# RWKV-7 hybrid layer: the triangular inverses of two head pairs share their visits to TensorE

## The chip, the cores and the metric

The kernel runs on one core of a Trainium2 chip. The metric is device time in microseconds for one launch. Three runs of the kernel before took 983.35, 985.12 and 985.98 us; the median is 985.12. Its engines are named as in the profile: PE is TensorE (PEld its weight loads), DVE is VectorE, ACT is ScalarE, POOL is GpSimd, SP is the engine that issues most transfers.

## What is computed

One layer of a hybrid decoder, for a prompt of 512 tokens and 8 x 8 sampled tokens (576 columns in all): an RWKV-7 branch and a differential-attention branch on the same normalised input, gated and merged, then a squared-ReLU MLP and a last norm. The change touches the RWKV branch alone. In the reference that branch is a recurrence over tokens on a 64 x 64 state for each of 8 heads:

```python
def step(S, inp):
    r_t, w_t, k_t, v_t, a_t, b_t = inp
    sa = jnp.einsum('bhij,bhj->bhi', S, a_t)
    S = S * w_t[:, :, None, :] + sa[..., None] * b_t[:, :, None, :] + v_t[..., None] * k_t[:, :, None, :]
    return S, jnp.einsum('bhij,bhj->bhi', S, r_t)
...
S, ys = lax.scan(step, S0.astype(jnp.float32), xs)
...
m = gate_a * (o_a @ lp['w_br_a']) + gate_b * (o_b @ lp['w_br_b'])
x = x + m @ lp['w_out']
hn = rmsnorm(x, lp['g_ffn'], NORM_EPS)
x = x + jnp.square(jax.nn.relu(hn @ lp['w_up'])) @ lp['w_down']
```

The kernel takes the tokens in chunks of 64. Within a chunk the recurrence is a triangular system, so for each chunk and head a 64 x 64 unit triangular matrix has to be inverted.

## The kernel before

The eight heads are four head pairs, hp 0 to 3; two heads of a pair lie on the upper and the lower 64 partitions. Pairs 0 and 1 are the first group, 2 and 3 the second; `e` is hp % 2. A group's recurrence over eight chunks is `chain(0)` or `chain(1)`, which needs the inverses of both its pairs.

`rwkv(hp)` is a generator in stages: the set-up up to the masked products A (ABR), then the transposes (SVU, KBt, pI), then the inverse, then what follows the chain. `run(...)` at the end of the phase advances these generators by one stage for each number it is given.

The inverse of a pair works on 9 chunks (8 of the prompt, one of the sampled tokens), as 32 x 32 blocks on the diagonal of the array. It makes four steps l = 1 to 4. Each has a visit with the products pW (from DM and X), an ACT copy W<-pW, a visit with the products pZ (from Y and W), a DVE sum X<-X,pZ and a DVE transpose Y<-X. Steps 1 and 2 take 36 products a visit (9 chunks by 4 blocks), steps 3 and 4 take 32. Two visits of 16 products, pWc and pC, then join the 32 x 32 blocks to the 64 x 64 inverse TT. A product of 32 x 32 in float32 stands as two records of PE and two of PEld in the trace. So a pair makes ten visits, one after the other, and each waits for what ACT or DVE made of the visit before.

To give TensorE work meanwhile, dense products wait in the list `waiting`: the streams of the big projections (ps_z for the RWKV inputs, ps_g for the gates, ps_brb for the attention branch), 128 x 128 weights by 288 or 296 columns. `take(n)` emits n of them, `fill(n)` does so behind the last product written, and `blocks()` took 9 behind each visit of a pair's inverse. They get a late priority, and the scheduler places them after what is due; `tc.issue_after(ins)` ties an instruction behind another on its engine.

Products of the inverse go to the one bank of `tbank`; `bank` is a pool of three banks that the set-up, the transposes and the outputs use. Lines that matter: `mm` (L72) records all these products, `act` is L58, `tt` L61; the transposes of the inverse are L894 and L918; the chain's products are L1021.

## Time and profile before

| what | before |
|---|---|
| median of three runs | 985.12 us |
| the profiled execution | 984.4 us |
| its span | 982.6 us |
| granted TensorE clock | 0.996 |
| DVE busy | 676.1 us, 69% of the span |
| ACT busy | 507.2 us, 52% |
| inverses of the first group, first to last product | 206.5 to 279.4 us |
| inverses of the second group | 381.9 to 431.3 us |

The page gives busy time by engine, the span in slices, the DMA queues and the chain of work that ended last. The trace can be asked for the instructions in order of time (the timeline), for what an engine waited for (the waits view), and for busy time and numbers of instructions in a stretch (the windows). "Issue" in a bracket means that an engine stood idle and nothing in the profile released it. A name such as pZ<-W,Y is the tile written and the tiles read.

### The profile page before, as it was taken

To read this page: it belongs to the slowest core of one execution; us is meant where nothing else is said; L and a number is where in the kernel's file an instruction comes from. 1 tells how busy PE (TensorE), PEld (TensorE's weight loads), DVE (VectorE), ACT (ScalarE), POOL (GpSimd) and SP (SyncE) were. 2 spreads that over 40 slices of the span, in tenths; PEclk is the share of its full clock that TensorE was granted. 3 is DMA by queue.
4 is the path that set the end of the run, shared out by engine and by line. 5 is a ranking of instruction groups with operands and counts; after the bars stand their busy time and mean duration, and the time that the engine had idled before them with its cause. 6 is when DMAs were issued, how large, how long until landed. Compare 5 with 4: busy or idle time off the path is not lost.

```text
span 982.6 us, 24623 instructions
## 1 busy us (share of the span) xinstructions
PE 951.1 (97%) x10120; PEld 898.2 (91%) x10120; DVE 676.1 (69%) x1427; ACT 507.2 (52%) x1120; POOL 72.8 (7%) x181
## 2 busy tenths in 40 slices
PE   8999999999999998999999999999999999999996
PEld 8999989887978997878899999999999999999996
DVE  6698566875556848354787989966666666666744
ACT  6576455565345464543354767444444444444732
POOL 2611100100010210001300000000000000000001
PEclk9999999999999999999999999999999999999998
DMA  7422663201212225221477532222222232220402
GB/s 267 141 71 72 207 222 118 86 26 45 67 57 77 94 88 190 70 83 58 173 239 234 179 121 86 87 86 87 86 87 87 90 93 93 92 86 23 140 1 97
DMA packets 50833, 105.75 MB, mean 108 GB/s; under 512 B 6066, under 2 KB 8114, under 8 KB 50594
## 3 DMA queue, kind: packets, MB, share of 16 engines
q1 hardware_dynamic: 47442, 96.95, 30.6%
q0 software_dynamic: 1648, 5.35, 1.6%
q10 hardware_dynamic: 1632, 1.89, 0.6%
q8 instruction: 79, 1.29, 0.5%
q14 instruction: 32, 0.26, 0.1%
HBM read 89.38 MB, written 14.78 MB: 106 GB/s over the span
## 4 chain that ended last, share of the span: by engine, by line
PE 56%; DVE 2%; ACT 1%; DMA 1%; issue 1%; POOL 0%; DVEq 0%
PE ps_dn L72 20%; PE ua L1261 5%; PE ux L1261 5%; PE ps_wo L72 4%; PE ps_g L72 4%; PE ps_brb L72 3%; PE ps_bra L72 3%; PE uc L1261 3%; PE ub L1261 3%; PE ud L1261 2%; PE pch L1021 2%; DMA raw_dn<-in_w_down_dram 1%; PE pW L72 1%; PE pZ L72 0%; DVE ya L61 0%
## 5 line engine op out<-in xcount | busy, mean ns | idle before, releaser
L72 PE MATMUL ps_dn<-q,hi_dn 128*128 128x288 f32 x768 | 154.7, 296 | 0.0
L72 PEld LDWEIGHTS ps_dn<-q,hi_dn 128*128 128x128 f32 x768 | 122.8, 188 | 1.5
L72 PE MATMUL ps_dn<-q,lo_dn 128*128 128x288 f32 x384 | 113.2, 295 | 0.0
L72 PE MATMUL ps_g<-xh,hi_g 128*128 128x288 f32 x256 | 77.7, 303 | 1.0 <-DVE gg L61 1.0
L72 PE MATMUL ps_g<-xh,lo_g 128*128 128x288 f32 x256 | 78.5, 307 | 0.0
L72 PE MATMUL ps_g<-xl,hi_g 128*128 128x288 f32 x256 | 78.2, 305 | 0.0
L72 PEld LDWEIGHTS ps_dn<-q,lo_dn 128*128 128x128 f32 x384 | 72.0, 188 | 0.0
L72 PE MATMUL ps_z<-xh,lo_z 128*128 128x288 f32 (+1 forms) x224 | 69.7, 311 | 0.0
L72 PE MATMUL ps_z<-xl,hi_z 128*128 128x288 f32 (+1 forms) x224 | 67.2, 300 | 0.0
L72 PE MATMUL ps_z<-xh,hi_z 128*128 128x288 f32 (+1 forms) x224 | 67.1, 299 | 0.0
L61 DVE TENSOR_TENSOR ya<-ya,ps_dn 128x288 f32<-128x288 f32 x96 | 43.3, 451 | 27.6 <-PE ps_dn L72 27.5
L58 ACT ACTIVATE hi_dn<-raw_dn 128x512 fp32r<-128x512 f32 x48 | 30.1, 628 | 56.2 <-PE ps_dn L72 56.1
L58 ACT ACTIVATE c<-c 128x288 f32<-128x288 f32 x112 | 48.7, 439 | 9.4 <-DVE c L61 7.7
L1261 PE MATMUL ux<-h_t,hi 128*128 128x288 f32 x256 | 52.4, 297 | 0.0
L1261 PE MATMUL ua<-h_b,hi 128*128 128x288 f32 x256 | 52.2, 296 | 0.0
L72 PEld LDWEIGHTS ps_g<-xh,hi_g 128*128 128x128 f32 x256 | 48.2, 188 | 2.5 <-issue 1.4
L72 PEld LDWEIGHTS ps_g<-xl,hi_g 128*128 128x128 f32 x256 | 48.2, 188 | 1.8 <-issue 0.5
L58 ACT ACTIVATE hi<-a 128x1024 fp32r<-128x1024 f32 (+1 forms) x32 | 27.1, 846 | 43.3 <-PE ps_dn L72 34.9
L72 PEld LDWEIGHTS ps_g<-xh,lo_g 128*128 128x128 f32 x256 | 48.1, 188 | 1.4
L72 PE MATMUL ps_dn<-q,w 128*128 128x320 f32 (+1 forms) x336 | 46.6, 298 | 0.8 <-DVE fin L61 0.8
L72 PEld LDWEIGHTS ps_dn<-q,w 128*128 128x128 f32 x336 | 45.3, 190 | 1.2 <-DVE fin L61 1.1
L61 DVE TENSOR_TENSOR lo<-s,hi 128x1024 fp32r<-128x1024 f32 x32 | 39.2, 1224 | 10.4 <-ACT hi L58 10.3
(390 smaller groups left out, 2730.6 us busy)
## 6 DMA issues: line engine op xcount, KB each, us to landing
a<-in_w_up_dram SPq DMA_DIRECT2D x32, 512.0 KB, 3.3
raw_dn<-in_w_down_dram SPq DMA_DIRECT2D x64, 256.0 KB, 2.8
raw_g<-in_w_in_dram SPq DMA_DIRECT2D x32, 256.0 KB, 3.1
raw_z<-in_w_in_dram SPq DMA_DIRECT2D x28, 256.0 KB, 2.9
gt_d<-gg SPq DMA_DIRECT2D x16, 288.0 KB, 2.8
g<-gt_d SPq DMA_DIRECT2D x16, 288.0 KB, 3.7
kp<-in_ktab_dram SPq DMA_DIRECT2D x16, 256.0 KB, 3.5
vp<-in_vtab_dram SPq DMA_DIRECT2D x16, 256.0 KB, 3.5
```

The source lines that it names most:

```text
L58: ring["act"] = AE.activation(out=out, in_=in_, func=func, **kw)
L61: ins = (eng or VE).tensor_tensor(out=out, in0=a, in1=b, op=op)
L72: ring["mm"] = PE.matmul(out=out, lhsT=lhsT, rhs=rhs, start=start, stop=stop)
L1021: ring["mm"] = PE.matmul(out=ps[rows, e], lhsT=lhs, rhs=rhs, start=first and e == 1, stop=True, skip_group_check=True)
L1261: ring["mm"] = PE.matmul(out=ps[:, :288], lhsT=l[:, k], rhs=hb[blk][:, h, k], start=start and i == 0, stop=i == 11, skip_group_check=skip)
```

## The change

The inverse leaves `rwkv` and becomes a generator of its own, `inverse(...)`, which yields after each visit. `rwkv` only makes it, at the end of its transposes. `invert(*steps)` advances the inverses of the pairs named in each step by one visit and then emits 9 dense products behind the last small one. With `(0,)` a visit is of pair 0 alone; with `(0, 1)` both pairs' products are written one behind the other. `tied` puts each product of the second pair behind the first pair's last one. The second pair's products use `bank`, not `tbank`.

For each group the steps are four for the even pair alone, then the odd pair's set-up, then seven with both, then four for the odd pair. The even pair has no products left in the seventh, so six visits are shared: pW of step 3 with pW of step 1 and so on to pC with pZ of step 3. The dense products taken between the two set-ups are 136 in the first group, which were 146; behind pWc and pC, too, nine are now taken.

```diff
+    visit = {}
+
+    def tied(*args):
+        with tc.issue_after(visit["last"].ins) if visit.get("last") else nullcontext():
+            last = mm(*args)
+        visit["lead"] = visit.get("lead") or last
+
+    def inverse(own, e, hp, dn, ST, KBt, ABR, pc):
+        tb = tbank if e == 0 else bank
...
+        def blocks(ps, lhs, rhs, n):
+            for ci in range(n):
+                for g in range(4):
+                    gs = slice(32 * g, 32 * g + 32)
+                    tied(ps[gs, ci * 32:ci * 32 + 32], lhs[gs, ci], rhs[gs, ci])
+            return ps[:, :n * 32].rearrange("p (c s) -> p c s", c=n)
+
+        for l in range(1, 5):
...
+            pW = blocks(tb(f"pW{hp}{l}"), DM, X, n)
+            yield
+            act(W[:, :n], pW)
+            pZ = blocks(tb(f"pZ{hp}{l}"), Y, W, n)
+            yield
+            tt(X[:, :n], X[:, :n], pZ, ADD)
...
+    def invert(*steps, dense=9):
+
+        for step in steps:
+            visit.clear()
+            for hp in step:
+                lead = visit.pop("lead", None)
+                if lead is not None:
+                    visit["last"] = ring["mm"]
+                next(pair[hp // 2]["inv", hp % 2], None)
+            with tc.issue_after(ring["mm"].ins):
+                take(dense)
+
...
-            act(W[:, :n], blocks(tbank(f"pW{hp}{l}"), DM, X, n))
-            tt(X[:, :n], X[:, :n], blocks(tbank(f"pZ{hp}{l}"), Y, W, n), ADD)
...
-        own[e] = ST, KBt, TT, ABR, pc
+        own["inv", e] = inverse(own, e, hp, dn, ST, KBt, ABR, pc)
         yield
...
     run(0, 0)
     take(101)
-    run(0, 1, 1)
-    take(146)
-    run(1)
+    invert(*[(0,)] * 4)
+    run(1, 1)
+    take(136)
+    invert(*[(0, 1)] * 6, *[(0, 1)], *[(1,)] * 4, dense=9)
     chain(0)
     run(0, 1, 2)
     take(310)
     run(2, 3)
     take(85)
-    run(2, 0, 1, 3)
+    invert(*[(2,)] * 4)
+    run(0, 1, 3)
     take(18)
-    run(3)
+    invert(*[(2, 3)] * 7, *[(3,)] * 4, dense=9)
```

On TensorE the first two visits of head pair 1 stood alone before, in the first group (pW and pZ are the small products, ps_z the dense ones):

```order
L72 MATMUL ps_z_1_3952<-xl,hi_z_1_3947 128x296
L72 MATMUL pW_4012<-X_4004,DM_1_4009 32x32 x36
L72 MATMUL ps_z_1_3952<-xh,lo_z_1_3948 128x296
...
L72 MATMUL ps_z_0_4074<-xl,hi_z_0_4066 128x288
L72 MATMUL pZ_4082<-W_1_4011,Y_4003 32x32 x36
L72 MATMUL ps_z_0_4074<-xh,lo_z_0_4067 128x288
```

The same two visits of pair 1 on TensorE now, with pair 0's third step in front of each (its W is W_3, its X and Y are X_3098 and Y_3097):

```order
L72 MATMUL ps_z_1_3685<-xl,hi_z_1_3680 128x296
L72 MATMUL pW_3736<-X_3098,DM_3_3733 32x32 x32
L72 MATMUL pW_3783<-X_3776,DM_1_3780 32x32 x36
L72 MATMUL ps_z_1_3685<-xh,lo_z_1_3681 128x296
...
L72 MATMUL ps_z_0_3845<-xl,hi_z_0_3837 128x288
L72 MATMUL pZ_3853<-W_3_3735,Y_3097 32x32 x32
L72 MATMUL pZ_3887<-W_1_3782,Y_3775 32x32 x36
L72 MATMUL ps_z_0_3845<-xh,lo_z_0_3838 128x288
```

Nine dense products stand between two visits in both orders; a visit now holds 68 products in a row where it held 36.

On VectorE, behind the first visits of pZ of pair 1, the order before was (X1 and Y1 are pair 1's; numbers behind a tile's name tell pair and step, DM the masked factor of a coming step):

```order
L61 TENSOR_TENSOR X1_4004<-X1_4004,pZ11_4082 128x288
L918 STREAM_TRANSPOSE Y1_4003<-X1_4004 128x288
L61 TENSOR_TENSOR DM1_4_4341<-DT1_3997,cst_sb_75 128x256
L61 TENSOR_TENSOR X1_4004<-X1_4004,pZ12_4180 128x288
L61 TENSOR_TENSOR Z11_4060<-ps_z11_0_4074,R1_108 128x288
```

and is now, with pair 0's X0 and Y0 in the same burst:

```order
L61 TENSOR_TENSOR X0_3098<-X0_3098,pZ03_3853 128x256
L790 STREAM_TRANSPOSE Y0_3097<-X0_3098 128x256
L61 TENSOR_TENSOR X1_3776<-X1_3776,pZ11_3887 128x288
L790 STREAM_TRANSPOSE Y1_3775<-X1_3776 128x288
L61 TENSOR_TENSOR DM1_3_4128<-DT1_3769,cst_sb_75 128x256
```

The sum and the transpose of pair 1 now stand behind those of pair 0, two sums and two transposes to a visit.

## The prediction

> **What bounds the kernel now.** I read the page first: the busy row, the chain, the DMA queues.

> ```profile
> PE 951.1 (97%) x10120; PEld 898.2 (91%) x10120; DVE 676.1 (69%) x1427; ACT 507.2 (52%) x1120; POOL 72.8 (7%) x181
> PE 56%; DVE 2%; ACT 1%; DMA 1%; issue 1%; POOL 0%; DVEq 0%
> q8 instruction: 79, 1.29, 0.5%
> ```

> TensorE is busy for 97% of the span and is what the chain is made of. So an edit moves the time only if TensorE does its fixed list of products in less time, or stands idle for less. The third row becomes important further down.

> Then the timeline of TensorE around single visits of the 32x32 products, since the change is about those. Columns: start, duration, what ran, how many, and in brackets the idle time ahead of it.

> ```profile
> 415.04 0.29 PE L72 MATMUL ps_g<-xh,hi_g 128*128 128x288 f32 x1
> 415.26 0.82 PE L72 MATMUL pW<-X,DM 32*32 32x32 f32 x72
> 416.01 0.41 PE L72 MATMUL ps_g<-xl,hi_g 128*128 128x288 f32 x1
> 416.26 0.29 PE L72 MATMUL ps_g<-xh,lo_g 128*128 128x288 f32 x1
> 416.39 0.29 PE L72 MATMUL ps_g<-xh,hi_g 128*128 128x288 f32 x1
> ...
> 417.18 0.29 PE L72 MATMUL ps_g<-xh,hi_g 128*128 128x288 f32 x1
> 417.40 0.75 PE L72 MATMUL pZ<-W,Y 32*32 32x32 f32 x65
> 418.77 0.26 PE L72 MATMUL pZ<-W,Y 32*32 32x32 f32 x7 [0.61 <-issue]
> 418.96 0.40 PE L72 MATMUL ps_g<-xl,hi_g 128*128 128x288 f32 x1
> ```
> ```profile
> 422.20 0.29 PE L72 MATMUL ps_g<-xh,hi_g 128*128 128x288 f32 x1
> 422.43 0.75 PE L72 MATMUL pZ<-W,Y 32*32 32x32 f32 x64
> 423.11 0.40 PE L72 MATMUL ps_g<-xl,hi_g 128*128 128x288 f32 x1
> 423.35 0.30 PE L72 MATMUL ps_g<-xh,lo_g 128*128 128x288 f32 x1
> ```
> ```profile
> 227.52 0.30 PE L72 MATMUL ps_z<-xl,hi_z 128*128 128x296 f32 x1
> 227.75 0.69 PE L72 MATMUL pC<-Y,Wc 32*32 32x32 f32 x32
> 228.37 0.40 PE L72 MATMUL ps_z<-xh,lo_z 128*128 128x296 f32 x1
> 228.61 0.30 PE L72 MATMUL ps_z<-xh,hi_z 128*128 128x296 f32 x1
> ```

> Dense products start 0.13 us apart (416.26 to 416.39; nine take 1.2 us). From the last dense start before a visit to the second dense start after it: 1.22 us with 72 records of small products (36 products, two records each), 1.15 us with 64. Eight records make the difference of 0.07, so one costs 0.00875 us. Of the 1.15 us, 64 records are 0.56 and the two dense steps 0.27; **0.32 us is the visit itself**, the price of leaving the dense stream and coming back. The visit of pC takes 1.09: less 0.27 and 0.32, its 32 records (other corners of the array) cost 0.50 us.

> **A second limit.** Inside the visit at 417.40 TensorE stops after 65 records and nothing releases it but "issue". I asked the waits view for all of these, and the windows between their ends:

> ```profile
> PE pZ L72 <- issue: 1.9, 3, 1.0
> ...
> 387.31:391.07 3.76, 2.74 (x142) 2.44 (x139) 2.23 (x6) 0.74 (x2) 0.00 (x0) 1.00 0.51 163
> 415.42:418.77 3.35, 2.73 (x146) 2.44 (x139) 0.43 (x1) 0.41 (x1) 0.00 (x0) 1.00 0.31 84
> 422.77:426.43 3.66, 3.37 (x149) 2.78 (x135) 2.47 (x5) 2.01 (x5) 0.00 (x0) 1.00 0.28 92
> 216.64:219.63 2.99, 2.99 (x130) 2.50 (x128) 2.83 (x6) 1.33 (x3) 0.00 (x0) 1.00 0.02 5
> ```
> ```profile
> 391.07:418.77 27.70, 26.33 (x765) 23.69 (x765) 10.68 (x22) 14.58 (x39) 0.00 (x0) 1.00 0.24 71
> 418.77:426.43 7.66, 7.37 (x255) 6.37 (x255) 4.00 (x8) 3.47 (x8) 0.00 (x0) 1.00 0.15 46
> 265.94:268.97 3.03, 3.03 (x129) 2.65 (x130) 1.24 (x3) 0.00 (x0) 0.00 (x0) 1.00 0.02 5
> ```
> ```profile
> q8 instruction: 1, 0.02, 5.8%
> ```

> The counts in brackets are records of TensorE and of its weight loads. Between the ends of the gaps at 391.07 and 418.77 lie 765 + 765 of them, six times 256 within the records cut at the edges; between 418.77 and 426.43, 255 + 255, twice 256. And 79 instruction packets against 20,240 records on the page are 256 records each. So TensorE's program arrives in blocks of 256, and it stops at a block's edge when the next has not come. The last row is of the DMA view for 388.5 to 389.8 us: one packet, 5.8% of 16 engines over 1.3 us, 1.2 us long; the gap it belongs to ended at 391.07, 1.3 us after that window. The first four windows each run from one edge to the next, where TensorE waited: a refill took 3.76, 3.35, 3.66 and 2.99 us. The fifth, 3.03 us, is a block passed without a gap, so its refill took at most that. Nothing in the traces shows two refills under way at once. Mean of the five: 3.36 us.

> **The change part by part.** The profiled execution took 984.4 us (span 982.6), 0.7 under the median of 985.12.

> *Fewer visits.* Ten visits a head pair, 40, become 28: in each group four alone, six shared, four alone. Twelve fewer at 0.32 us: **-3.8 us**. No product goes away. The chain and the head-pair set-up meet other dense products than before (the order has three fewer excursions to the chain, a few more to transposes and A blocks); I take 0, within 1 us both ways.

> *Waits on other engines.* Of the dependency waits of the inverses only one of the two of pWc, head pair 0's, falls into a shared visit and goes:

> ```profile
> PE pW L72 <- DVE X L61: 1.6, 2, 1.2
> PE pWc L72 <- DVE X L61: 0.4, 2, 0.2
> ```

> The 1.6 us are in visits that stay alone, the first steps of head pairs 0 and 2, with the same VectorE work ahead of them. **-0.2 us**; -2.0 if they all go, and 0 if this one only moves.

> *Tied products.* The small products of a visit stand in one run already (x72, x64), so the ties cost and save 0. The second pair's products use the shared banks, not the one bank kept for them; nobody waits for a bank in the rows, so 0.

> *Supply of the shared stretch.* This is the term that decides. Four shared visits hold 32 + 36 products, 136 records on TensorE and as many weight loads; two hold 16 + 32, 96 and 96. With nine dense products (18 records) between them the stretch has 4x272 + 2x192 + 5x18 = 1562 records, 6.1 blocks. Unhindered it takes 4x(0.32 + 136x0.00875) + 2x(0.32 + 0.50 + 64x0.00875) + 5x1.2 = 14.8 us, **2.43 us a block: faster than any refill seen**. Alone, a visit of 64 and its dense products are 146 records in 2.1 us, 3.6 us a block, just above the 3.36; that is why only a few gaps are in the trace now. At the start of a stretch the current block (half of it on average) and the next one are there; 4.6 blocks have to be waited for, each 3.36 - 2.43 = 0.93 us: 4.3 us a group, **+8.6 us** for both. At 2.99 us it is 5.2, at 3.76 it is 12.2, and 0 if a refill can come in 2.43.

> *The gaps of today.* The three issue gaps sum to 1.9 us of idle; each costs some 0.2 more than its idle (the visit at 417.40 lasts 1.56 us to the next dense product, against 0.75 for the one at 415.26: 0.81 for 0.61 idle), and a fourth, inside this row, costs 0.2 against the 0.75 of its like:

> ```profile
> 218.97 0.97 PE L72 MATMUL pZ<-W,Y 32*32 32x32 f32 x64
> ```

> Together 2.7 us over 40 lone visits; 16 remain alone, so 1.1 stays and **-1.6 us** goes.

> Sum: -3.8 - 0.2 + 8.6 - 1.6 = **+3.0 us**: 984.4 becomes 987.4, 0.2% above the median. A measurement tells about 0.3%, 3 us, from no change.

> **The rivals.**

> *The program keeps up.* If the gaps are a thing of single visits (a late packet now and then) and not of the rate, they shrink with the visits, 2.7x12/40 = 0.8 us. Then 984.4 - 3.8 - 0.2 - 0.8 = 979.6. For it: TensorE passes most visits without a gap. Against it: the gaps stand exactly on multiples of 256, and no block in these windows passes in under 2.99 us. [...]

> *The refill is slow.* The forecast hangs on 3.36. With 3.76, as in the window with the busiest DMA engines (share 0.51), the stretch costs 12.2: 984.4 - 3.8 - 0.2 - 1.6 + 12.2 = 991.0, slower. Slower by 0.3% than the median, 988.1, means +3.7 us, reached when 9.2 blocks times (refill - 2.43) is 9.3: **from 3.44 us a refill**. Two of the four gaps are above that, and their mean is 3.44. Against it: gaps pick out slow refills, and the fifth window had 3.03 without one.

> *VectorE is late in the shared visits.* After a shared pZ it adds and transposes for two pairs in a row:

> ```profile
> 391.42 0.46 DVE L61 TENSOR_TENSOR X<-X,pZ 128x288 f32<-128x288 f32 x1 [1.88 <-PE pZ L72]
> 391.91 0.48 DVE L918 STREAM_TRANSPOSE Y<-X 128x288 f32<-128x288 f32 x1
> ```

> About 0.85 us for each, end to end. The first pair's sum is due 0.6 us after its products and the next visit comes some 2 us after them; the second's sum is due some 1.4 us after its own, and its products stand 0.6 us further inside the next visit. Other work of 0.7 us in between fits; a longer burst would cost up to the 1.2 us that it cost once before (the pW row). That wait would stand in place of a supply gap, since the refill goes on meanwhile: at four such bursts, in the first group alone, 979.6 + 4x1.2 = 984.4, no change.

> **How the numbers follow.** The forecast, supply-bound at about 3.36 us, 987.4: 0.37. VectorE late, 984.4: 0.05. Refill slow, 991.0: 0.35. Program keeps up, 979.6: 0.23. So faster 0.23, same 0.42, slower 0.35. The likeliest alone would lie in 984 to 988 (refill 2.99 to 3.44: 984.0 to 988.1). The range takes in both neighbours: 979.6 to 991.0.

> **What would show it.** Right: 28 visits; in the waits view issue ahead of pZ, pW or pC rises from 1.9 us to about 8 in sum, with gaps inside shared visits, 256 records from one to the next and 3 to 3.8 us apart; lone visits as today. The excess of a shared visit free of gaps is 0.32 us beyond its records. Wrong: shared visits of 1.2 us (136 records) following each other every 2.7 us with no gap, or gaps that name VectorE's X or ScalarE's W; or gaps that stand elsewhere than 256 apart, then supply is not their cause. If the chain starts with more idle time than today, the shared stretch pushed work into it that I counted at 0.

## The result, and the profile after

| | before | after |
|---|---|---|
| median | 984.66 us (983.26 to 985.98, 8 runs) | 988.38 us (987.49 to 993.98, 8 runs) |
| ratio | | 1.0049, 95% interval 1.0030 to 1.0069 |
| the profiled execution, its span | 984.4 us, 982.6 us | 993.98 us, 992.1 us |
| its granted TensorE clock | 0.996 | 0.987 |

The change makes the kernel 3.7 us slower. The profiled execution of after is the slowest of its eight; the other seven had clocks of 0.989 to 0.992. A second profiled execution of the same kernel (e8 below) took 986.83 us at a clock of 0.994, and both are used.

The page of after: busy time and number of instructions by engine, and the granted clock in 40 slices of 24.8 us.

```profile
PE 956.3 (96%) x10120; PEld 905.3 (91%) x10120; DVE 674.7 (68%) x1427; ACT 507.0 (51%) x1120; POOL 74.3 (7%) x181
PEclk9999999999999999889999999999999999999998
```

The list of products is the same (10,120), but TensorE is busy 5.2 us longer with it, and two slices at 397 to 446 us, where the second group's shared visits are, show a lower clock.

The waits view of after (engine, tile and line; what it waited for; us in total, times, longest):

```profile
PE pZ L72 <- issue: 5.8, 5, 1.5
PE ps_g L72 <- issue: 2.3, 1, 2.3
PE pW L72 <- issue: 2.2, 2, 1.3
PE pA L72 <- DVE ABR L61: 2.2, 4, 1.0
...
PE pW L72 <- DVE X L61: 1.3, 2, 1.1
...
PE pWc L72 <- issue: 0.9, 1, 0.9
```

Issue has gone from 2.4 us (1.9 and 0.5 in the chain) to 11.2. No row says that a shared visit waits for X or W: the 1.3 us for X are again in steps 1 and 2 of pairs 0 and 2, which stay alone.

The windows view of after, from the end of one issue gap to the end of the next. Columns: stretch, length, then busy time and records of PE, PEld, DVE, ACT, POOL, granted clock, DMA share, GB/s.

```profile
253.37:257.38 4.01, 2.74 (x130) 2.44 (x129) 1.68 (x4) 0.38 (x1) 0.60 (x3) 1.00 0.07 24
257.38:261.38 4.00, 2.74 (x129) 2.42 (x128) 0.43 (x1) 0.41 (x1) 0.00 (x0) 1.00 0.01 4
...
405.47:409.20 3.73, 2.75 (x129) 2.43 (x129) 2.83 (x6) 1.02 (x2) 0.00 (x0) 1.00 0.30 75
409.20:414.02 4.82, 2.50 (x128) 2.22 (x128) 0.85 (x2) 0.80 (x2) 0.00 (x0) 0.93 0.39 121
414.02:417.59 3.57, 2.46 (x127) 2.08 (x128) 1.36 (x3) 0.42 (x1) 0.00 (x0) 0.50 0.02 5
```

Some 128 products' records (127 to 130) and 128 weight loads (127 to 129) stand between two neighbouring gaps of a stretch: one block of 256. There are nine such gaps, five in the first shared stretch and four in the second; within a stretch the refills took 4.01, 4.00, 3.92, 4.01 and 3.73, 4.82, 3.57 us. In these rows TensorE has 2.5 to 2.75 us of work to a block and stands idle for the rest. In the second row DVE and ACT are nearly empty and the DMA share is 0.01, and the refill is no shorter: no other engine's work sets it.

The instruction packets of the same trace show how a refill passes. Within these stretches the next packet starts only 1.1 to 2.4 us behind the end of a gap, it takes 0.9 to 1.0 us, and the next gap ends 1.3 to 1.5 us behind its landing. The refill of 4.82 us and that of 3.57 differ in the first of these parts: 2.39 us against 1.12.

The timeline of TensorE in after, second shared stretch (start, duration, what, how many, idle time ahead of it):

```profile
407.89 0.33 PE L72 MATMUL pW<-X,DM 32*32 32x32 f32 x16
409.20 1.25 PE L72 MATMUL pW<-X,DM 32*32 32x32 f32 x120 [0.98 <-issue]
...
411.40 0.29 PE L72 MATMUL ps_g<-xh,hi_g 128*128 128x288 f32 x1
414.02 0.61 PE L72 MATMUL ps_g<-xl,hi_g 128*128 128x288 f32 x1 [2.33 <-issue]
414.56 1.93 PE L72 MATMUL pZ<-W,Y 32*32 32x32 f32 x126
417.59 0.37 PE L72 MATMUL pZ<-W,Y 32*32 32x32 f32 x10 [1.10 <-issue]
417.89 0.61 PE L72 MATMUL ps_g<-xh,lo_g 128*128 128x288 f32 x1
418.30 0.44 PE L72 MATMUL ps_g<-xh,hi_g 128*128 128x288 f32 x1
418.54 0.44 PE L72 MATMUL ps_g<-xl,hi_g 128*128 128x288 f32 x1
```

The visits hold 136 records as the change says, and are cut by the gaps. After the gap of 2.33 us everything is slower: dense products start 0.24 us apart (418.30 to 418.54) where it was 0.13. The windows view of after gives the stretches with a granted clock of a half:

```profile
362.13:365.55 3.42, 3.42 (x12) 2.71 (x11) 0.00 (x0) 0.80 (x2) 1.87 (x10) 0.50 0.08 28
413.33:430.40 17.07, 15.27 (x422) 13.80 (x423) 4.30 (x9) 5.11 (x12) 0.00 (x0) 0.50 0.02 4
```

20.5 us of it, with 18.7 us of busy time. A dense step takes 0.24 instead of 0.13 us there, so 0.45 of that busy time, some 8 us, is lost. Before has no such stretch up to 974.9 us, where one begins that lasts to its end; in after the like begins at 986.8 us.

**Where the time went.** From the first pW to the first ps_bra both kernels do the same list of products. The windows view of before, and of after:

```profile
206.49:505.62 299.13, 285.31 (x4848) 250.09 (x4848) 186.86 (x418) 143.18 (x343) 29.63 (x66) 1.00 0.29 95
```
```profile
207.41:516.26 308.85, 289.69 (x4849) 255.65 (x4849) 185.72 (x418) 143.10 (x343) 32.38 (x71) 0.97 0.29 91
```

The difference of 9.7 us is all of the difference in the span (9.5). Busy time is +4.4; without the 8.4 us of the slow clock it is **-4.0, put down to the twelve visits**. Idle time is +5.3, of which issue is +8.8 and all other waits -3.5. The second execution, in the windows view of e8:

```profile
207.23:509.18 301.95, 284.60 (x4849) 251.28 (x4849) 186.46 (x418) 143.39 (x343) 31.83 (x71) 0.99 0.29 94
413.10:419.90 6.80, 6.26 (x122) 5.85 (x122) 1.31 (x3) 2.45 (x6) 0.00 (x0) 0.50 0.02 5
```

The row of the visits is a remainder, and it can be off by 2 us. In e5 below, which has the changed code with all 40 visits alone, the windows view of the phase is

```profile
206.25:505.74 299.49, 288.71 (x4849) 251.74 (x4849) 186.67 (x418) 143.30 (x343) 31.20 (x67) 0.99 0.29 93
```

Its busy time is 3.4 us above that of before, and its one half-speed window explains only 1.5 of that.

| us, against the profile of before | forecast | after | after again (e8) |
|---|---|---|---|
| visits | -3.8 | -4.0 | -3.5 |
| issue (supply, less today's gaps) | +7.0 | +8.8 | +7.4 |
| other waits | -0.2 | -3.5 | -3.9 |
| clock at a half | 0 | +8.4 | +2.8 |
| sum of the phase | +3.0 | +9.7 | +2.8 |

The rows of the table are worked out as above (e8: 0.45 x 6.26 = 2.8; busy -0.7 without it -3.5; idle 17.35 against 13.82, issue 9.8 against 2.4). They are not independent: in the slow stretch of after no gap is left behind 417.59, though visits of the same sizes had gaps at full speed in the first group.

### The profile page after: what moved, and what is told of

It is laid out like the page before. It is cut to its first block, busy times and chain, and to the rows that moved or that the text cites. A ratio compares the mean times of both kernels' runs of the same rounds, so it can differ in the third digit from the quotient of the medians.

```text
span 992.1 us, 24619 instructions
## 1 busy us (share of the span) xinstructions
PE 956.3 (96%) x10120; PEld 905.3 (91%) x10120; DVE 674.7 (68%) x1427; ACT 507.0 (51%) x1120; POOL 74.3 (7%) x181
## 3 DMA queue, kind: packets, MB, share of 16 engines
q8 instruction: 79, 1.29, 0.5%
## 4 chain that ended last, share of the span: by engine, by line
PE 80%; DVE 6%; issue 6%; ACT 5%; DMA 1%; POOL 1%; DVEq 0%; SPq 0%; ACTq 0%; POOLq 0%
PE ps_dn L72 20%; PE ps_g L72 8%; PE ps_z L72 6%; PE ua L1287 5%; PE ux L1287 5%; PE ps_wo L72 4%; PE ps_k L72 3%; PE ps_bra L72 3%; PE uc L1287 3%; PE ub L1287 3%; PE ud L1287 2%; PE pch L1045 2%; PE ps_brb L72 2%; PE ps_q L72 2%; PE ps_v L72 2%
## 5 line engine op out<-in xcount | busy, mean ns | idle before, releaser
L72 PE MATMUL ps_dn<-q,hi_dn 128*128 128x288 f32 x768 | 154.7, 296 | 0.0
L72 PEld LDWEIGHTS ps_dn<-q,hi_dn 128*128 128x128 f32 x768 | 122.8, 188 | 1.4
L72 PE MATMUL ps_dn<-q,lo_dn 128*128 128x288 f32 x384 | 113.2, 295 | 0.0
L72 PE MATMUL ps_g<-xl,hi_g 128*128 128x288 f32 x256 | 79.3, 310 | 2.3 <-issue 2.3
L72 PE MATMUL ps_g<-xh,lo_g 128*128 128x288 f32 x256 | 80.5, 315 | 0.0
L72 PE MATMUL ps_g<-xh,hi_g 128*128 128x288 f32 x256 | 79.7, 311 | 0.0
L72 PEld LDWEIGHTS ps_dn<-q,lo_dn 128*128 128x128 f32 x384 | 72.1, 188 | 0.0
L72 PE MATMUL ps_z<-xh,lo_z 128*128 128x288 f32 (+1 forms) x224 | 69.6, 311 | 0.0
L72 PE MATMUL ps_z<-xl,hi_z 128*128 128x288 f32 (+1 forms) x224 | 67.6, 302 | 0.0
L72 PE MATMUL ps_z<-xh,hi_z 128*128 128x288 f32 (+1 forms) x224 | 67.0, 299 | 0.0
L61 DVE TENSOR_TENSOR ya<-ya,ps_dn 128x288 f32<-128x288 f32 x96 | 43.3, 451 | 27.6 <-PE ps_dn L72 27.5
L72 PEld LDWEIGHTS ps_g<-xl,hi_g 128*128 128x128 f32 x256 | 49.9, 195 | 3.5 <-issue 2.6
L72 PEld LDWEIGHTS ps_g<-xh,hi_g 128*128 128x128 f32 x256 | 49.9, 195 | 2.4 <-issue 1.3
L72 PEld LDWEIGHTS ps_g<-xh,lo_g 128*128 128x128 f32 x256 | 49.6, 194 | 1.7 <-issue 0.2
L72 PE MATMUL ps_dn<-q,w 128*128 128x320 f32 (+1 forms) x336 | 46.6, 298 | 0.4 <-DVE fin L61 0.4
L61 DVE TENSOR_TENSOR lo<-s,hi 128x1024 fp32r<-128x1024 f32 x32 | 39.2, 1224 | 10.3 <-ACT hi L58 10.3
L72 PEld LDWEIGHTS ps_dn<-q,w 128*128 128x128 f32 x336 | 45.3, 190 | 0.8 <-DVE fin L61 0.7
```

The costliest lines, as they stand in the source:

```text
L61: ins = (eng or VE).tensor_tensor(out=out, in0=a, in1=b, op=op)
L72: ring["mm"] = PE.matmul(out=out, lhsT=lhsT, rhs=rhs, start=start, stop=stop)
```

## The experiments

Theory: the sharing saves the visits and loses them again, since the program's blocks of 256 records come too slowly for the shared stretch. Rivals: the loss is in the code and the dense products moved around the visits; the program keeps up; VectorE is late.

**e1: the changed code with all visits alone.** What is different from after:

```diff
-    invert(*[(0,)] * 4)
+    invert(*[(0,)] * 11)
     run(1, 1)
-    take(136)
-    invert(*[(0, 1)] * 6, *[(0, 1)], *[(1,)] * 4, dense=9)
+    take(94)
+    invert(*[(1,)] * 11)
...
-    take(85)
-    invert(*[(2,)] * 4)
+    take(51)
+    invert(*[(2,)] * 11)
     run(0, 1, 3)
-    take(18)
-    invert(*[(2, 3)] * 7, *[(3,)] * 4, dense=9)
+    invert(*[(3,)] * 11)
```

> The changed code with every visit of one head pair alone again: 40 visits, nine dense products behind each, the dense products between the set-ups reduced so that their sum is as before. Theory (the program arrives in blocks of 256 records, 3 to 3.8 us each, and the shared stretch asks for them every 2.4 us): as before the change, 984.7 within 1.5, issue gaps of about 2 us in sum, granted clock 0.995 or more. Rival (the loss is in the code around the visits: the second pair's bank, the generators' order, the dense products taken between the set-ups): stays near the changed kernel, 987 or more.

Measured: 990.72 us, ratio 1.0060 (1.0043 to 1.0077), no faster than the change itself. A miss for the theory as I had put it. The waits view of e1:

```profile
PE ps_g L72 <- DVE lo_g L61: 1.9, 1, 1.9
PE pA L72 <- ACT ST L58: 1.8, 1, 1.8
...
PE pW L72 <- issue: 0.9, 1, 0.9
```

Issue is as small as in before, but two long waits are new. The one for ST stands in the set-up of the second group, from which my edit took 34 dense products (85 became 51). The one for lo_g does not come of that, as e3 below keeps the 85 and has it too. The clock is at a half in two windows, at 353 and 367 us. All this confounds the run.

**e5: the same with the cover left in place.** Against e1:

```diff
-    take(94)
+    take(74)
...
-    take(310)
+    take(296)
...
-    take(51)
+    take(85)
```

> All visits alone as in e1_lone, but with the 85 dense products between the set-ups of pairs 2 and 3 left in place (e1_lone took 51 there, and TensorE then waited 1.8 us for ScalarE's ST and 0.8 for VectorE's ABR ahead of pair 3's A blocks); 34 fewer are taken elsewhere. Theory (e1_lone lost by its own dense placement, not by the code around the visits): 985 to 987. Rival (generators, bank or nine dense products behind pWc and pC cost by themselves): 989 or more again.

Measured: 984.99 us, ratio 1.0004 (0.9989 to 1.0019). The generators, the other bank and the moved dense products cost nothing in sum. Two parts of the change are not in e5: the ties have nothing to tie where no visit has two pairs, and the odd pair's set-up stands behind the even pair's visits again. Both are in e2 below, which is level with before as well. Beside e1 (0.56% or 5.5 us apart, by the ratios) e5 also suggests what such cover is worth, though two other counts differ. The waits view of e5 has issue at 0.6 and 0.3 us for the small and the dense products; the loss of the change is in the sharing.

**e4: the products of the first group's inverses written twice, in the order of before.** It has no sharing: the first group's visits stay alone, sixteen of them with 64 or 72 products and four with 16. The second copy writes the same results.

```diff
+            for ci in range(n if hp < 2 else 0):
+                for g in range(4):
+                    gs = slice(32 * g, 32 * g + 32)
+                    last = mm(ps[gs, ci * 32:ci * 32 + 32], lhs[gs, ci], rhs[gs, ci])
```

> The kernel before, with the pW and pZ products of the first group's 16 lone visits each written twice over (the same sums again, same result). Nothing is shared, VectorE and ScalarE have their work as before. Theory: each visit with its nine dense products is 274 to 306 records, 3.8 us at 3.36 us a block against 2.1 us now, so 16 x 1.7 = +27 us, 1012, with gaps 256 records apart. Rival (no supply limit; only TensorE's time for the records counts): 16 x 0.59 = +9.5 us, 994.

Measured: 1013.7 us in one run; the rival without a limit is 20 us off. The waits and the windows between gaps of e4:

```profile
PE pZ L72 <- issue: 10.2, 9, 2.2
PE pW L72 <- issue: 5.1, 5, 1.5
```
```profile
218.12:221.94 3.82, 2.10 (x127) 1.82 (x128) 0.00 (x0) 0.00 (x0) 0.00 (x0) 1.00 0.02 4
229.15:233.43 4.28, 2.78 (x129) 2.46 (x130) 0.87 (x2) 0.63 (x1) 0.00 (x0) 1.00 0.21 65
...
286.45:289.90 3.45, 1.27 (x128) 1.17 (x128) 0.00 (x0) 0.00 (x0) 0.00 (x0) 0.77 0.02 5
```

The gaps stand one block apart here too, and a block of only 1.27 us of work still took 3.45 us. With DVE and ACT at 0.00 and a DMA share of 0.02 in the first and the last row, neither VectorE nor DMA traffic sets the pace. The supply limit is shown, without any sharing.

**e2, e3, e6: more dense products behind a shared visit.** With 22, a visit and its dense products are 272 + 44 records in 0.32 + 1.19 + 22 x 0.13 us, 3.6 us a block, about a refill; 15 lies between. The products come from the stocks ahead of the set-ups. e2, and the lines in which e3 and e6 differ from it:

```diff
-    take(136)
-    invert(*[(0, 1)] * 6, *[(0, 1)], *[(1,)] * 4, dense=9)
+    take(116)
+    invert(*[(0, 1)] * 6, dense=22)
+    invert(*[(0, 1)], *[(1,)] * 4)
...
-    take(310)
+    take(232)
...
-    take(85)
+    take(55)
...
-    invert(*[(2, 3)] * 7, *[(3,)] * 4, dense=9)
+    invert(*[(2, 3)] * 6, dense=22)
+    invert(*[(2, 3)], *[(3,)] * 4)
```
```diff
 e3
+    invert(*[(0, 1)] * 6, dense=15)
...
+    take(274)
 e6
+    take(80)
+    invert(*[(0, 1)] * 6, dense=24)
...
+    take(230)
```

In all three the attention branch's products join the list ahead of pair 2's visits; e3 keeps 136 and 85, e6 keeps 85. The second group's shared visits take the same number as the first's.

> Shared visits as in the change, but 22 dense products behind each of the six shared ones (nine elsewhere; as many fewer are taken in the set-ups). A shared visit and its dense products are then 316 records in 1.50 + 2.93 = 4.4 us, 3.6 us a block. Theory: the gaps in the shared stretch go (under 1.5 us of issue in all), the clock stays at 0.995, and the twelve saved visits show: 984.7 - 3.8 - 0.2 - 1.6 = 979 within 1.5. Rival (TensorE's clock falls because so many 32x32 products stand in one run, gaps or not): granted clock stays near 0.99 and the time at 984 or more. Rival (the program keeps up anyway and the loss is elsewhere): 988, as changed.

> The same with 15 dense products: 302 records in 3.5 us, 2.97 us a block. Theory: each block short by some 0.4 us, 4.8 blocks a group, about 4 us of issue gaps in the shared stretches and 1 elsewhere; 984.7 - 5.6 + 3.8 = 983 if the clock holds, 985 if it falls for a while. Rivals as for 22: 984 or more with a clock near 0.99, or 988.

> Six shared visits with 24 dense products behind each (320 records in 4.7 us, 3.75 us a block, near the refills of 3.6 to 4.0 seen in the changed kernel), and those 85 left in place (e2_dense22 took 55 and waited 3.7 us for ScalarE's ST). Theory: issue under 1.5 us, no 3.7 us wait: e2_dense22's 983.8 less about 3, 981 within 1.5. Rival (the clock's half-speed windows, not the gaps, hold the time up): granted clock 0.991 as in e2_dense22 and 983 or more.

Measured: e2 983.76 us, ratio 0.9988 (0.9976 to 1.0000); e3 991.11, 1.0062 (1.0039 to 1.0085); e6 990.44, 1.0066 (1.0041 to 1.0091). The waits view of e2, of e3 and of e6:

```profile
PE pA L72 <- ACT ST L58: 3.7, 1, 3.7
...
PE ps_g L72 <- issue: 1.2, 1, 1.2
```
```profile
PE pW L72 <- issue: 3.7, 4, 3.0
...
PE pF L72 <- POOL vm L61: 2.0, 1, 2.0
PE ps_g L72 <- DVE lo_g L61: 2.0, 1, 2.0
PE ps_bra L72 <- ACT oab L58: 1.5, 1, 1.5
```
```profile
PE pZ L72 <- issue: 4.7, 3, 2.0
PE pK L76 <- ACT SVU L58: 3.2, 2, 2.7
```

The gaps answer to the number of dense products: issue in the phase is 11.2 us with 9, 5.0 with 15, 1.7 with 22. In e6, with 24, it is 4.7, most of it in two gaps of some 2 us, one of them in a lone visit; why there, is not settled. The times miss by 5 to 9 us. Single waits grow where products were borrowed: pA for ST in e2 (55 instead of 85), lo_g and vm in e3, pK for SVU in e6. But all waits other than issue are 10.7, 11.4 and 11.1 us in the phase, against 10.6 in before. More was lost to the clock: by the same 0.45, the half-speed stretches in the phase cost 3.6 us in e2, 4.4 in e3 and 3.1 in e6. In e2 they lie at 350 and 367 us, in the set-up of the second group, so its clock of 0.991 doesn't speak for the rival of many 32x32 products in one run. In e6 the stock is also used up at the end: from the first ps_bra to the first ps_wo it takes 29.9 us against 25.7. So 22 dense products remove most of the supply gaps, but this kernel hasn't got them to spare: e2 is level with before, no better.

**e7: all visits of both pairs shared, 20 dense products each,** 21 visits instead of 28; pair 0 waits for pair 1's set-up.

```diff
-    run(0, 0)
-    take(101)
-    invert(*[(0,)] * 4)
-    run(1, 1)
-    take(136)
-    invert(*[(0, 1)] * 6, *[(0, 1)], *[(1,)] * 4, dense=9)
+    run(0, 0, 1)
+    take(75)
+    run(1)
+    take(20)
+    invert(*[(0, 1)] * 11, dense=20)
...
-    invert(*[(2, 3)] * 7, *[(3,)] * 4, dense=9)
+    invert(*[(2, 3)] * 11, dense=20)
```

> Both pairs of a group inverted step by step together, all visits shared (21 instead of 40), 20 dense products behind each: 328 records in 4.2 us, 3.3 us a block. Theory: 19 visits saved, 6.1 us, but each block short by 0.3 to 0.7 of a refill over some 13 blocks a group: 984.6 - 6.1 - 1.6 + 26 x 0.5 = 990. Rival (visits alone count, supply does not): 977.

Measured: 998.25 us, ratio 1.0143 (1.0107 to 1.0178). Issue is 7.3 us, since 20 dense products give 3.3 to 3.6 us a block by the same sum, not quite enough, and the clock is at a half for 24 us in seven windows. The direction was expected, the size not: the ACT waits of the phase are 5.5 us against 2.3 in before, and the stretch behind ps_bra takes 31.6 us instead of 25.7 for want of dense products.

**e8: the changed kernel once more,** for the clock.

> The changed kernel once more, for a second profile: about 988; issue gaps of 8 to 11 us in the shared stretches, again 256 records apart, and a granted clock of 0.991, that is half speed in three or so windows of 3.4 us. If the half-speed windows follow the gaps they lie inside or just behind the shared stretches; if they belong to the set-up of pairs 2 and 3 they lie at 350 to 375 us as in e1_lone and e2_dense22.

Measured: 986.83 us, with 9.8 us of issue gaps and a clock of 0.994. The slow stretch lies at 413 us again, at the second gap of its pair of 1.49 and 1.91 us, and not at 362. The clock fell with the gaps there in both executions, and stayed down for 6.8 us here and 17.1 in the other.

**e9 and e10: one group shared, the other alone,** each the change with e5's lines for one group (and 288 and 318 for 310).

```diff
 e9
-    invert(*[(2,)] * 4)
+    invert(*[(2,)] * 11)
     run(0, 1, 3)
-    take(18)
-    invert(*[(2, 3)] * 7, *[(3,)] * 4, dense=9)
+    invert(*[(3,)] * 11)
 e10
-    invert(*[(0,)] * 4)
+    invert(*[(0,)] * 11)
     run(1, 1)
-    take(136)
-    invert(*[(0, 1)] * 6, *[(0, 1)], *[(1,)] * 4, dense=9)
+    take(74)
+    invert(*[(1,)] * 11)
```

> Only the first group's visits are shared; the second group's twenty are alone, as in e5. Theory (the loss of the change is the supply gaps of both shared stretches, and the clock falls with the gaps of the second one): issue in the first stretch 5 to 6 us, the second near 1; visits -1.9, today's gaps -0.8, other waits -1.5, so +1 to +2 us over before, 985.5 to 987, with a mean clock of 0.995 or more and full speed between 380 and 440 us. Rival (the clock falls wherever visits are shared): half-speed windows at 250 to 275 us as well, the clock at 0.993 and about 988. Rival (the first group costs nothing): 984.5.

> Only the second group's visits are shared; the first group's twenty are alone, as in e5. Theory: issue of 4 to 5 us in the shared stretch, near 1 elsewhere; visits -1.9, today's gaps -0.8, other waits -1.5, so within 1 us of before by the gaps alone, and 2 to 4 us more from a granted clock that falls to half within or just behind a gap of that stretch: 986.5 to 989, mean clock 0.990 to 0.994. Rival (the fall of the clock has nothing to do with the stretch): full speed from 400 to 440 us, 984.5 to 985.5. The changes in e9 and e10 should add up to that of the whole change, +3.7 us.

Measured: e9 987.66 us, ratio 1.0022 (1.0009 to 1.0036); e10 994.99, ratio 1.0103 (1.0084 to 1.0121), against a before of 985.66. The first group alone costs 2 us, as expected, with a clock of 0.991 to 0.998 (median 0.996). But the profiled execution has a half-speed window at 254.3 us, behind a gap of 1.77: the clock fell in the first group too, behind a gap of that length. e10 is a miss, for a reason outside the sharing. The waits and the VectorE timeline of e10:

```profile
PE pA L72 <- DVE ABR L61: 4.3, 2, 3.6
PE pW L72 <- issue: 3.4, 2, 2.4
```
```profile
383.79 0.76 DVE L61 TENSOR_TENSOR obh<-ob,obh 128x576 fp32r<-128x576 f32 x1 [3.61 <-ACT obh L58]
384.47 0.68 DVE L61 TENSOR_TENSOR ABR<-pA,cst_sb 128x512 f32<-128x512 f32 x1
```

Here VectorE got a piece of the attention branch (obh, which waits for ACT and that for a load of ob) in front of ABR, and TensorE stood 3.6 us in the set-up of pair 2. The clock fell to a half 1.2 us later, for 6.8 us. The half-speed stretches of its phase, another of 6.8 us at 359 among them, cost 7.5 us by the same 0.45. One more window, at 417.1 us, stands at a gap of 2.43 us in a shared visit, so the rival of full speed there fell. But the two groups can't be added up; what the second one costs alone is left open.

**What the clock answers to.** Up to 520 us, the half-speed stretches of all these executions are single, double or fivefold windows of 3.41 us, and within an execution they sit on one grid: in after 413.33 - 362.13 = 51.20 = 15 x 3.413, in e7 the five starts are 34, 12, 7 and 29 windows apart. I laid that grid over the eleven profiled executions that have such a stretch, from 200 to 520 us, and counted TensorE's idle time in each window at full speed. Of 20 windows with 1.64 us of idle or more, 18 were followed by one at half speed; of 964 with less, 7, and none of the more than a hundred with 0.5 to 1.6 us. What TensorE waited for made no difference: issue (2.33 us in after), ACT (3.7 in e2, 2.7 in e6), VectorE (3.6 in e10) or GpSimd (2.0 in e3). The window ahead of the fall, in the windows view of after, and the one in e10:

```profile
409.92:413.33 3.41, 1.77 (x66) 1.50 (x54) 0.79 (x2) 0.80 (x2) 0.00 (x0) 1.00 0.44 126
```
```profile
382.97:386.39 3.42, 1.18 (x32) 1.05 (x32) 2.55 (x5) 0.68 (x1) 0.00 (x0) 1.00 0.70 270
```

1.77 and 1.18 us busy of 3.41: about half idle is the edge in these executions. It was chosen after the fact: after's own window, with 1.64 us of idle, is the one of the 18 with the least. The edge is a finding over executions, not an experiment that set the idle time. The seven other falls all lie at 350 to 367 us, in the set-up of the second group, with less than 0.5 us idle; their cause is open.

## Why the prediction was right, and where not

- **Fewer visits, -3.8 us: right.** The price of 0.32 us, read from lone visits, holds for shared ones: in after, a shared visit of 136 records without a gap (at 248.24 us) takes 1.78 us from dense to second dense, and 0.27 + 0.32 + 136 x 0.00875 = 1.78. The remainders of -4.0 and -3.5 agree with it more closely than they can be trusted: against e5's busy time they would be -5.9 and -5.4.
- **Ties, bank, moved chain and set-up at 0: not contradicted.** e5 (1.0004) has the new bank and generators; the ties and the moved set-up are only in kernels that share visits, and of these e2 is level with before.
- **Waits on other engines, -0.2 us: mis-sized, -3.5 and -3.9.** The kind was right (no new wait in shared visits); I counted only the inverses' own waits. VectorE's alone fell from 7.2 to 4.8 us in the phase. That the supply gaps give VectorE and ScalarE the time to catch up fits, but was not tried apart; e5, with 1.0 us of issue, has 1.7 us less of other waits too, so the gaps can't be all of it.
- **Supply, +8.6 us, less 1.6: right in kind, and near in size** (+8.8 and +7.4 against +7.0 net). Nine gaps, one block apart, in the shared visits, and e4 shows the same limit without sharing. Two parts were off against each other, and the nearness is luck to that extent: the refill took 4.0 us on average in after (seven gaps) and 3.7 in e8, not 3.36; and a block's own work is 2.5 to 3.0 us in after's seven windows from gap to gap, not 2.43, as a gap also adds some time to the visit that it cuts (0.81 us for 0.61 of idle at 417.40 in before), and the slow clock (0.93 and 0.50) to the last two. The block and a half put as there at the start of a stretch was an estimate; with it 4.6 gaps a group were due, and five and four came.
- **VectorE late: fell.** No shared visit waits for X or W in after or e8.
- **The program keeps up: fell.** e4 and e2 show it from both sides: 17.5 us of issue gaps with more records to a visit, 1.7 with more dense work between.
- **Refill slow, 3.76 us:** the refills were that slow (3.7 us on average in e8) or slower (4.0 in after), and by the line that the prediction drew between the two (3.44 us a refill, 988.1) this rival came rather than the forecast, just across the line in time (988.4). The time is still not 991.0, since the block's own work and the other waits took part of it back.
- **The step that was missing: the granted clock.** I took every duration at full speed. In the two profiled executions 2.8 us (e8) and 8.4 us (after) came from half-speed windows. With a clock of 0.989 to 0.992 in the other seven runs, against 0.996 in the profile of before, the term is in the median too. That the sum came out within 1 us of the median is luck: two things that it lacked nearly cancel, in e8 +2.8 us of the clock and -3.7 of other waits.

## What to carry to other kernels

Count instruction records per microsecond before bunching small products: here 256 records of TensorE and its weight loads took 4.0 us on average in after and 3.7 in e8 where TensorE waited for them, and 136 + 136 records of 32x32 products wanted some 22 dense products behind them (1.7 us of issue in e2), not 9 (11.2 us). Dense filler is a fixed stock: taken from a set-up, it uncovered waits there (for ST 1.8 us in e1 and 3.7 in e2, for SVU 3.2 in e6). And look at the granted clock window by window: idle time of TensorE that reached half of a 3.4 us window was paid twice here in 18 of 20 cases, the second time as a window or more at half speed.
